# Constant products in TensorE's planned waits, a norm's sums on TensorE, and inverse square roots as powers on GpSimd

## The chip, the cores and the metric

The kernel runs on one NeuronCore of a Trainium2 chip. The core has five engines that run their own instruction queues in order and wait for one another by semaphores: TensorE (PE in the profile, with its weight loads listed as PEld), VectorE (DVE), ScalarE (ACT), GpSimd (POOL) and SyncE (SP), which here only issues DMAs. The metric is the device time of one execution in microseconds; the kernel before took 3143.68 us, the median of 3 runs from 3141.57 to 3146.34.

## What is computed

Two transformer blocks run one after the other on 512 tokens of 1024 features (the second block puts 16 learned tokens in front, so 528). All is float32. The first block has depth 2, each layer made of a gated feed-forward (FFN), a mixer of sliding-window attention and retention, and another FFN, every one followed by a layer norm. The second block has depth 1: FFN, a mixer of differential attention and of attention over tokens picked by an index score, and an FFN, with RMS norms ahead of each. Cut to what the change touches:

```
x = layer_norm(ALPHA * x + 0.5 * swiglu_ffn(x, ...), ln3_g, ln3_b)        # last of block 1
h = concatenate([meta_tokens, x]);  h = h + 0.5 * swiglu(rmsnorm(h, ffn1_norm), ...)   # first of block 2
layer_norm: (x - mean) * rsqrt(var + 1e-5) * g + b
rmsnorm:     x * rsqrt(mean(x * x) + 1e-6) * g
multiscale_retention:  o = (o - mu) * rsqrt(var + 1e-6)          # per head, 64 wide
mixer 2: qa, ka = rmsnorm per 64;  c, q_lat = rmsnorm per 256;  o_a = rmsnorm per 128
```

## The kernel before

**Layout.** Activations lie as 128 partitions (features) by tokens, `Z[128, 8, 528]`: 8 feature blocks, and the token axis is worked in two halves. Every float32 product with a weight is made of three products in the faster fp32r format (`mm3`): the weight and the activation are each split into a high and a low part, high*high, high*low and low*high add up in PSUM. The weights come by DMA one 128x1024 tile at a time (`wraw`), ScalarE writes the high part (`wsplit`), VectorE or GpSimd subtracts to get the low one. In the FFNs some products use a scheme with 7 products instead of 8 of half-size blocks, whose operands are sums of blocks (`turned`, `sums`).

**Who sets the order.** The Python program that writes the instructions keeps a plan: a clock for every engine (`plan.t["P"]` is TensorE's), a cost for every instruction (`Plan.COST`, and in `Engine` 0.1085 us or 0.000422 us per column for an fp32r product) and the end of every access to every tile. Work that hangs on other engines is written as jobs, Python generators that yield whenever their next step has to wait. The main program issues products; after each it calls `tick()`, which issues the weight preparation and every job step whose time has come on TensorE's planned clock (`run_due`). Where the main program can't go on (no free PSUM bank in `have`, or a condition in `until`), nothing is due, and the planned clock of TensorE is set forward to the next due time: the plan foresees a wait there. Since every engine runs its queue in order, the plan fixes the order of all instructions for good; on the chip an instruction starts when its semaphores allow.

**PSUM.** There are 8 banks in three rooms: `acc` (4), `s` (2) and `m` (2).

**The norms.** `Norm` gathers the sums of a norm while the products that make `Z` are still running. For each feature block and half, `_acc` squares `Z` on ScalarE and adds to the partial sums in SBUF. The kind "ln" keeps two sums (x and x*x), "rms" one. The kind "both" stands between the two blocks: a layer norm followed at once by an RMS norm, whose sum of squares is worked out from five sums (x, x*g*g, x*g*b, x*x, x*x*g*g) so that the tokens need only one pass; `wts` holds g*g and g*b. `stats` adds up over partitions with products with `ones` in TensorE, gets the inverse square roots, `bcast` spreads them over partitions with products with the unit matrix (`m<-identf,st`), and `apply` scales the 8 feature blocks (two VectorE products with PSUM, ScalarE for g and b, a further VectorE product with the RMS gain, and the split into high and low parts `x`).

**The inverse square root.** `rsqrt` is an integer guess of the bit pattern and two polynomial steps, 7 small VectorE instructions in a row, each on the one before; the constant KAPPA folds a scale into what it is given. It is used in the norms' `stats` (tile `st`, 2 or 3 columns), in retention's `group_norm` (8 columns), and in the second mixer for `qa` and `ka` (8 columns), the compressed keys (1), the latent queries (2) and the attention's output (4).

**Stages by time of the profile.** FFN 0 to 345 us, mixer 345 to 600, the first norm's hand-over to the next FFN 600 to 660, FFN to 945, FFN to 1300, mixer to 1595, hand-over to 1660, FFN to 1940, the "both" norm and the hand-over to block 2 from 1940 to 2090, FFN to 2345, second mixer 2425 to 2700, its output and norm to 2810, last FFN to the end.

Of the kernel before, what the change touches and what calls it, by code (L numbers as in the profile page):

```python
# [19 lines left out]
KAPPA = 13.375  # L20
R1, R2 = (-0.9039771828045722, 1.7085235438039765), (-4.244243335422951, 5.270893790588845)
# [4 lines left out]
MORE, TAIL = 1, 3  # L26
# [253 lines left out]
class Plan:  # L280
# [11 lines left out]
    def cost(self, e, name, n, reads, writes, kw, scalars):  # L292
        a, b = self.COST[e]
        if e == "S":
# [162 lines left out]
def build(ctx, tc, t, out, stop=None, dbg=None):  # L457
# [74 lines left out]
    V.memset(mean128, 1.0 / 128)  # L532
    ones = const.tile([128, 2], F32, name="ones")
# [83 lines left out]

    def until(done):
        while not done():
            W.advance()  # L620
            W.pump()
            if not run_due() and not done():
                plan.t["P"] = max(plan.t["P"], min(due(j) for j in eligible()))
# [32 lines left out]
    class Norm:  # L656
# [5 lines left out]
        def __init__(self, kind, halves, g=None, b=None, rms=None, xo=0):  # L662
# [3 lines left out]
            self.more = []  # L666
# [15 lines left out]
        def _acc(self, m, h):  # L682
# [30 lines left out]
            if self.kind == "both":  # L713
                add(self.more[2], q, 0)
# [14 lines left out]
        def z(self, m, *halves):  # L729

            if self.s2 is None:
                if self.kind == "both":
                    lt = main.tile([128, 4, 512], F32, name="lt", tag="V")
                    self.s1, self.s2 = lt[:, 0], lt[:, 1]
                    self.more = [lt[:, 2], lt[:, 3], have(tmps, (128, 512))]
# [20 lines left out]
        def stats(self, half):  # L756
# [6 lines left out]
            p = yield from want(ms, (128, 5, 3, 32))  # L763
            sums = [(j, u) for j, u in enumerate([self.s1, self.s2, *self.more]) if u is not None]
            for i, (c, w) in enumerate(tk):
                for j, u in sums:
                    PE.matmul(p[:w, j, i, 0:2], u[:, c:c + w], ones, start=True, stop=True)
            S1, S2, S1g, S1b, S2g = (p[:, j, 0:nt, 0] for j in range(5))
            if self.kind == "rms":
                if short < 128:  # L770
                    V.memset(v, 1.0)
                V.tensor_scalar(v[:, :full], S2[:, :full], KAPPA / 1024, KAPPA * 1e-6, op0=OP.mult, op1=OP.add)
                if full < nt:
                    V.tensor_scalar(v[:short, full:], S2[:short, full:], KAPPA / 1024, KAPPA * 1e-6, op0=OP.mult, op1=OP.add)
# [1740 lines left out]
```

## Time and profile before

| what | value |
| --- | --- |
| median of 3 runs | 3143.68 us |
| the profiled execution | 3140.53 us, span of its instructions 3138.8 us, so 1.7 us lie around the span |
| mean granted TensorE clock | 0.974 of full |
| TensorE busy | 3017.5 us, 96%, 20218 products |
| TensorE idle | 3138.8 - 3017.5 = 121.3 us |
| VectorE busy | 2240.9 us, 71% |
| ScalarE busy | 1368.0 us, 44% |
| GpSimd busy | 534.6 us, 17%, 360 instructions |
| share of the chain that ended last | PE 43%, DVE 8%, issue 3%, ACT 1% |

The granted clock has two levels, 1.2 and 2.4 GHz, shown as 0.5 and 1.0; a mean in between tells how much of a stretch was spent at each. A wait is shown at the end of a row as the idle time of the engine before the instruction and who ended it. An instruction of the program that multiplies float32 as it is (not fp32r) shows as two products in the trace: the program has 56 of `m<-ones,lt`, the trace 112.

### The profile page before, as it was taken

Reading aid. Unit: us, or ns where it says so; the run is one execution under the profiler, and the core shown is the slowest. Engines: PE = TensorE matmul, PEld = TensorE weight load, DVE = VectorE, ACT = ScalarE, POOL = GpSimd, SP = SyncE. Lnnn points to the kernel's source line nnn. Section 1 sums busy time; section 2 is a strip of 40 time slices with the busy share of each in tenths; the row PEclk is TensorE's granted clock in tenths of the full one; section 3 lists DMA queues with packets and bytes.
Section 4 is the critical chain, followed back from the end, with each engine's and each line's share of the span. In section 5 each row is a group of like instructions: output and inputs, shape, how many; then the busy total and the mean of one; then the engine's idle time right before and its main releaser. Section 6 shows DMA issues by size and latency. Waiting matters only on the chain.

```text
span 3138.8 us, 51092 instructions
## 1 busy us (share of the span) xinstructions
PE 3017.5 (96%) x20218; PEld 2739.3 (87%) x20218; DVE 2240.9 (71%) x4654; ACT 1368.0 (44%) x2517; POOL 534.6 (17%) x360
## 2 busy tenths in 40 slices
PE   8999999999999999999989999789999998999999
PEld 8999877789999999987779999789999677789997
DVE  6767655687677766775678668877675898577774
ACT  4444464354345433456344334243344345543342
POOL 1121222112212122022221221111102000212110
PEclk9999999999999999999999999899999997899999
DMA  4333221212323233311212323023332110122332
GB/s 145 108 101 103 87 89 61 74 61 95 102 101 102 95 101 102 127 61 61 68 48 84 105 101 128 22 72 99 101 108 89 56 58 21 34 78 97 101 101 88
DMA packets 75551, 269.71 MB, mean 86 GB/s; under 512 B 8445, under 2 KB 10533, under 8 KB 75184
## 3 DMA queue, kind: packets, MB, share of 16 engines
q1 hardware_dynamic: 73712, 261.65, 25.3%
q0 software_dynamic: 1024, 3.75, 0.4%
q8 instruction: 159, 2.61, 0.4%
q10 hardware_dynamic: 576, 1.05, 0.1%
q14 instruction: 80, 0.66, 0.1%
HBM read 264.30 MB, written 3.68 MB: 85 GB/s over the span
## 4 chain that ended last, share of the span: by engine, by line
PE 43%; DVE 8%; issue 3%; ACT 1%; POOL 0%; DMA 0%; DVEq 0%; ACTq 0%; POOLq 0%
PE acc L429 38%; PE m L429 2%; PE s L429 2%; DVE tmp L429 2%; DVE wsplit L429 1%; DVE Z L429 1%; DVE rsq L429 1%; DVE small L429 1%; DVE lt L429 1%; DVE sel L429 1%; ACT wsplit L429 0%; ACT tmp L429 0%; DVE turned L429 0%; DVE st L429 0%; POOL wsplit L429 0%
## 5 line engine op out<-in xcount | busy, mean ns | idle before, releaser
L429 PE MATMUL acc<-x,wsplit 128*128 128x256 f32 (+3 forms) x4248 | 607.7, 295 | 40.4 <-ACT x L429 17.8
L429 PEld LDWEIGHTS acc<-x,wsplit 128*128 128x128 f32 x4248 | 562.0, 194 | 60.1 <-ACT x L429 19.4
L429 ACT ACTIVATE wsplit<-wraw 128x1024 fp32r<-128x1024 f32 (+1 forms) x455 | 423.8, 947 | 384.0 <-PE acc L429 335.1
L429 PE MATMUL acc<-turned,wsplit 128*128 128x256 f32 (+1 forms) x4320 | 565.3, 283 | 8.6 <-DVE wsplit L429 6.3
L429 PEld LDWEIGHTS acc<-turned,wsplit 128*128 128x128 f32 x4320 | 541.0, 189 | 16.8 <-DVE wsplit L429 8.7
L429 DVE TENSOR_TENSOR wsplit<-wraw,wsplit 128x1024 fp32r<-128x1024 f32 (+1 forms) x376 | 402.3, 1074 | 132.1 <-ACT wsplit L429 130.1
L429 PE MATMUL acc<-H,wsplit 128*128 128x512 f32 (+2 forms) x2490 | 463.7, 339 | 5.0 <-DVE H L429 2.7
L429 PEld LDWEIGHTS acc<-H,wsplit 128*128 128x128 f32 x2490 | 380.3, 189 | 56.0 <-DVE H L429 4.8
L429 POOL TENSOR_TENSOR wsplit<-wraw,wsplit 128x1024 fp32r<-128x1024 f32 x79 | 193.5, 2449 | 1138.2 <-ACT wsplit L429 1030.2
L429 DVE TENSOR_TENSOR Z<-Z,acc 128x512 f32<-128x512 f32 (+2 forms) x295 | 165.7, 563 | 272.8 <-PE acc L429 272.0
L429 PE MATMUL acc<-wsplit,x 128*128 128x512 f32 (+3 forms) x1536 | 354.1, 381 | 0.0
L429 DVE TENSOR_TENSOR tmp<-tmp,acc 128x256 f32<-128x256 f32 (+1 forms) x570 | 238.7, 419 | 141.2 <-PE acc L429 133.8
L429 PEld LDWEIGHTS acc<-wsplit,x 128*128 128x128 f32 (+1 forms) x1536 | 261.4, 187 | 58.3 <-issue 1.2
L429 ACT ACTIVATE tmp<-acc 128x256 f32<-128x256 f32 (+4 forms) x282 | 110.0, 392 | 326.7 <-PE acc L429 313.0
L429 PE MATMUL acc<-H,turned 128*128 128x256 f32 (+2 forms) x1416 | 244.1, 327 | 0.0
L429 PEld LDWEIGHTS acc<-H,turned 128*128 128x128 f32 x1416 | 208.3, 191 | 20.6
L429 POOL TENSOR_TENSOR lent<-wraw,lent 128x1024 fp32r<-128x1024 f32 x45 | 110.9, 2464 | 595.3 <-ACT lent L429 572.7
L429 ACT ACTIVATE wsplit<-sums 128x1024 fp32r<-128x1024 f32 x90 | 95.3, 1059 | 236.7 <-DVE sums L429 236.3
L429 PE MATMUL acc<-x,lent 128*128 128x256 f32 (+1 forms) x1032 | 136.9, 281 | 0.0
L429 PEld LDWEIGHTS acc<-x,lent 128*128 128x128 f32 x1032 | 130.8, 188 | 2.4
L429 DVE TENSOR_TENSOR wsplit<-sums,wsplit 128x1024 fp32r<-128x1024 f32 x88 | 107.5, 1221 | 19.6 <-ACT wsplit L429 19.5
L429 DVE TENSOR_TENSOR sums<-wraw 128x512 f32<-128x512 f32 x173 | 119.4, 690 | 1.3
(327 smaller groups left out, 4133.3 us busy)
## 6 DMA issues: line engine op xcount, KB each, us to landing
wraw<-in_w_dram SPq DMA_DIRECT2D x489, 512.0 KB, 3.3
decay<-in_decay_dram SPq DMA_DIRECT2D x4, 512.0 KB, 4.9
vr<-vr POOLq DMA_DIRECT2D x1, 1536.0 KB, 8.1
Z<-in_x_dram SPq DMA_DIRECT2D x4, 256.0 KB, 6.2
Z<-in_x_dram SPq DMA_DIRECT2D x2, 512.0 KB, 12.5
tb<-vr POOLq DMA_DIRECT2D x2, 512.0 KB, 4.3
out_dram<-Z SPq DMA_DIRECT2D x4, 256.0 KB, 2.0
out_dram<-Z ACTq DMA_DIRECT2D x4, 256.0 KB, 2.0
```

Of the source, the lines that this page charges most:

```text
L429: r = f(*args, **kw)
```

## The change

Four things change.

- **Filled waits.** Where `have` or `until` set TensorE's planned clock forward, they now call `idle(upto)`. It takes a free PSUM bank and issues `n = wait * 0.8 / 0.118` products of the constant tile `minus` (128 rows by 256 columns, fp32r), whose result nobody reads, if n is at least 2. In all 491 of them in 40 places.
- **The "both" norm's sums.** `_acc` no longer adds five sums in SBUF. For every feature block, half and 128 tokens it makes two float32 products with `Z` and with its square as the stationary operand and four and two columns of `wts` as the moving one, adding up over the 8 feature blocks in one PSUM bank (`s`). `stats` reads the sums there, and the products with `ones` go for this norm.
- **rsqrt.** One GpSimd instruction, a power with exponent -0.5, in place of the 7 VectorE ones. KAPPA goes. In the plan it costs 0.4 + 0.156 us per column.
- **A yield behind rsqrt.** The jobs now give up their turn behind it, so that VectorE's next step of the job is issued when the plan says that the power is done.

```diff
-MORE, TAIL = 1, 3
+MORE, TAIL, WARM = 1, 3, 0.8
...
     def cost(self, e, name, n, reads, writes, kw, scalars):
         a, b = self.COST[e]
+        if kw.get("op") == OP.pow:
+            return 0.4 + 0.156 * n
...
             if not run_due():
-                plan.t["P"] = min([at] + [due(j) for j in eligible() if due(j) > now])
+                idle(min([at] + [due(j) for j in eligible() if due(j) > now]))
...
+    def idle(upto):
+
+        n = int((upto - plan.t["P"]) * WARM / 0.118)
+        rooms = [r for r in (ms, ss, accs) if r.open and r._at(r.open[0]) <= plan.t["P"]]
+        if n > 1 and rooms:
+            p = rooms[0].take((128, 512), F32)
+            for _ in range(n):
+                PE.matmul(p[:, :256], minus[:, 0:1].to_broadcast([128, 128]), minus[:, 0:1].to_broadcast([128, 256]),
+                          start=True, stop=True)
+            drop(p)
+        plan.t["P"] = max(plan.t["P"], upto)
...
     def rsqrt(v, n, rows=128, out=None):
 
-        y, q, a = (main.tile([128, n], F32, name="rsq", tag="rsq" + u, bufs=2)[:rows] for u in "yqa")
-        y = y if out is None else out
-        V.tensor_scalar(y.bitcast(I32), v.bitcast(I32), -0.5, float(0x5F3759DF), op0=OP.mult, op1=OP.add)
-        V.tensor_mul(q, y, y)
-        V.tensor_mul(q, q, v)
-        V.scalar_tensor_tensor(a, q, R1[0], q, op0=OP.add, op1=OP.mult)
-        V.scalar_tensor_tensor(q, q, R2[0], q, op0=OP.add, op1=OP.mult)
-        V.scalar_tensor_tensor(y, a, R1[1], y, op0=OP.add, op1=OP.mult)
-        V.scalar_tensor_tensor(y, q, R2[1], y, op0=OP.add, op1=OP.mult)
+        y = main.tile([128, n], F32, name="rsq", tag="rsq", bufs=6)[:rows] if out is None else out
+        G.tensor_tensor(y, v, power[:rows].to_broadcast([rows, n]), op=OP.pow)
         return y
...
+            if self.kind == "both":
+                q = yield from want(tmps, (128, n))
+                S.activation(q, z, AF.Square)
+                yield
+                for i, (t0, w) in enumerate(self.toks(h)):
+                    p = self.s2[:w, 2 * h + i]
+                    t0 -= c0
+                    PE.matmul(p[:, 0:4], z[:, t0:t0 + w], wts[:, m, 0:4], start=not self.begun, stop=m == 7,
+                              skip_group_check=True)
+                    self.begun.add(h)
+                    PE.matmul(p[:, 4:6], q[:, t0:t0 + w], wts[:, m, 0:2], start=False, stop=m == 7,
+                              skip_group_check=True)
+                drop(q)
+                self.taken[h] += 1
+                return
...
-            def add(d, a, col):
-                w = wts[:, m, col:col + 1]
-                if first:
-                    V.tensor_scalar(d[:, c0:c1], a, w, None, op0=OP.mult)
-                else:
-                    V.scalar_tensor_tensor(d[:, c0:c1], a, w, d[:, c0:c1], op0=OP.mult, op1=OP.add)
-
-            if self.kind == "both":
-                add(self.more[0], z, 0)
-                add(self.more[1], z, 1)
-            yield
-            if self.kind == "both":
-                add(self.more[2], q, 0)
+            yield
...
             rsqrt(v, nt, out=r)
             if self.kind != "rms":
+                yield
                 V.tensor_mul(mr, r, mu)
```

TensorE's queue at the end of the FFN ahead of block 2, the difference between the two programs; `m<-minus` are the constant products, `m<-Z,mean` is the mean of the first feature block, which the norm subtracts. The same two pieces stand at the end of the two FFNs before it.

```order
 L429 MATMUL acc<-x,wsplit 128x256 x12
 L429 MATMUL acc<-H,turned 128x512 x12
+L429 MATMUL m<-minus 128x256 x14
 L429 MATMUL acc<-H,wsplit 128x512 x24
+L429 MATMUL m<-minus 128x256 x7
 L429 MATMUL m<-Z,mean_94 128x512
```

Fourteen constant products now stand between the last down product of one chunk and the 24 products that need the last gated tile `H`, and seven ahead of the mean.

TensorE's queue at the "both" norm, before: the products that make the second half of `Z` stand on either side of the five sums' products with `ones` (4 on `lt` and 1 on `tmp` for each 128 tokens).

```order
L429 MATMUL acc<-H,wsplit 128x256 x24
L429 MATMUL acc<-tmp,minus 128x256
L429 MATMUL acc<-H,turned 128x256 x6
L429 MATMUL m<-ones,lt 128x2 x4
L429 MATMUL m<-ones,tmp 128x2
...
L429 MATMUL acc<-H,turned 128x256 x18
```

The same place now: the first of the 64 products with `wts` are put in between the products that make `Z`, as soon as the plan has a feature block ready.

```order
L429 MATMUL m<-Z,mean_94 128x512
L429 MATMUL acc<-H,wsplit 128x256 x21
L429 MATMUL s<-wts,Z 128x4
L429 MATMUL s<-wts,tmp 128x2
...
L429 MATMUL acc<-H,wsplit 128x256 x3
L429 MATMUL acc<-tmp,minus 128x256
```

They moved from one place behind each half into pairs strewn along the products of both halves, and there are 64 where 20 were.

VectorE's queue in the second mixer, before: the norm of a 128-token piece of `ka`, from the sum over squares (`TENSOR_REDUCE`) to the product with the result; `sel` are the index scores.

```order
L429 TENSOR_REDUCE small<-tmp 128x8
L429 TENSOR_SCALAR small<-small 128x8
L429 TENSOR_SCALAR rsq<-small 128x8
L429 TENSOR_TENSOR rsq<-rsq 128x8
L429 TENSOR_TENSOR rsq<-rsq,small 128x8
L429 SCALAR_TENSOR_TENSOR rsq<-rsq 128x8 x4
L429 TENSOR_TENSOR tmp<-acc,rsq 128x512
```

The first two such pieces now, on the same engine:

```order
L429 TENSOR_REDUCE small<-tmp 128x8
L429 TENSOR_SCALAR small<-small 128x8
L429 SCALAR_TENSOR_TENSOR sel_24648<-tmp,iw,sel_24648 128x528 x2
...
L429 TENSOR_TENSOR tmp<-acc,rsq 128x512
L429 MAX small<-sel_24646 128x8
L429 MATCH_REPLACE sel_24646<-small,sel_24646 128x272
```

Seven instructions are gone from between, and other work of VectorE stands there while GpSimd takes the power; two such pieces now run one in the other, and the bank `acc` is held until `tmp<-acc,rsq`. In this mixer TensorE's queue has 153 constant products, the largest groups 51 and 25, both among the `ka` and `va` products.

## Rows read from the trace of the kernel before

**Rows 1.** The page: busy time by engine, and the granted clock in 40 slices.
```profile
PE 3017.5 (96%) x20218; PEld 2739.3 (87%) x20218; DVE 2240.9 (71%) x4654; ACT 1368.0 (44%) x2517; POOL 534.6 (17%) x360
...
PEclk9999999999999999999999999899999997899999
```
**Rows 2.** Busy time by stretch: length, then PE, PEld, DVE, ACT, POOL, clock, DMA.
```profile
600.00:660.00 60.00, 51.24 (x336) 47.03 (x335) 49.34 (x132) 26.45 (x54) 11.32 (x8) 0.90 0.18 62
...
1660.00:1940.00 280.00, 279.19 (x1982) 261.75 (x1981) 201.73 (x315) 114.62 (x170) 53.01 (x28) 1.00 0.31 103
1940.00:2090.00 150.00, 120.66 (x837) 116.26 (x836) 122.74 (x310) 57.42 (x107) 20.70 (x16) 0.85 0.16 54
2425.00:2560.00 135.00, 125.23 (x638) 97.28 (x638) 116.75 (x319) 56.22 (x118) 6.39 (x3) 0.97 0.20 67
2560.00:2700.00 140.00, 124.21 (x668) 102.67 (x669) 112.52 (x411) 73.62 (x219) 15.43 (x15) 0.80 0.11 35
...
1595.00:1660.00 65.00, 56.10 (x413) 53.58 (x412) 57.82 (x166) 35.67 (x81) 13.84 (x12) 0.92 0.21 66
```
**Rows 3.** TensorE's waits from 1940 to 2090 us: total, times, longest.
```profile
PE s L429 <- ACT x L429: 8.4, 1, 8.4
PE acc L429 <- ACT tmp L429: 7.3, 2, 4.6
PE m L429 <- DVE lt L429: 6.3, 2, 4.6
PE acc L429 <- ACT x L429: 5.2, 1, 5.2
```
**Rows 4.** VectorE's groups by shape, 1955 to 2035 us: count, total, mean ns.
```profile
L429 DVE SCALAR_TENSOR_TENSOR lt<-Z,wts,lt 128x256 f32<-128x256 f32 x28 | 14.2, 547 | 0.0
...
L429 DVE SCALAR_TENSOR_TENSOR tmp<-tmp,wts 128x256 f32<-128x256 f32 x14 | 8.7, 624 | 0.0
...
L429 DVE TENSOR_TENSOR lt<-lt,Z 128x256 f32<-128x256 f32 x14 | 5.8, 412 | 0.0
L429 DVE TENSOR_TENSOR lt<-lt,tmp 128x256 f32<-128x256 f32 x14 | 5.8, 411 | 0.0
```
**Rows 5.** Timeline, the norm between the blocks: start, duration, what, count.
```profile
1970.09 2.99 PE L429 MATMUL acc<-H,wsplit 128*128 128x256 f32 x24
...
1971.36 2.81 POOL L429 TENSOR_TENSOR wsplit<-wraw,wsplit 128x1024 fp32r<-128x1024 f32 x1 [16.52 <-ACT wsplit L429]
...
1971.83 2.61 DVE L429 SCALAR_TENSOR_TENSOR tmp<-tmp,wts 128x256 f32<-128x256 f32 x1
...
1982.30 1.85 PE L429 MATMUL m<-ones,lt 128*128 128x2 f32 x8
...
2015.72 0.95 PE L429 MATMUL m<-ones,lt 128*128 128x2 f32 x8
```
**Rows 6.** Timeline of TensorE, the end of the first FFN.
```profile
326.68 5.07 PE L429 MATMUL acc<-H,wsplit 128*128 128x512 f32 x14 [1.37 <-DVE H L429]
```
**Rows 7.** The same at the end of the FFN ahead of block 2.
```profile
1945.33 3.51 PE L429 MATMUL acc<-H,wsplit 128*128 128x512 f32 x14 [0.18 <-DVE H L429]
1948.68 1.02 PE L429 MATMUL m<-Z,mean 128*128 128x512 f32 x2
```
**Rows 8.** The same at the start, and in the last FFN.
```profile
7.11 2.71 PE L429 MATMUL acc<-x,wsplit 128*128 128x256 f32 x11 [0.71 <-DVE x L429]
...
22.96 14.21 PE L429 MATMUL acc<-x,wsplit 128*128 128x256 f32 x118 [0.98 <-DVE wsplit L429]
...
3097.01 0.49 PE L429 MATMUL acc<-H,wsplit 128*128 128x512 f32 x1 [0.54 <-ACT H L429]
```
**Rows 9.** TensorE's waits from 2300 to 2425 us, the end of the fifth FFN.
```profile
PE acc L429 <- ACT H L429: 1.5, 1, 1.5
```
**Rows 10.** Timeline of VectorE, one inverse square root in the second mixer.
```profile
2462.77 0.17 DVE L429 TENSOR_SCALAR rsq<-small 128x8 int32<-128x8 int32 x1
...
2464.12 0.69 DVE L429 TENSOR_TENSOR tmp<-acc,rsq 128x512 f32<-128x512 f32 x1
```
**Rows 11.** TensorE's waits from 2425 to 2560 us, the first half of the second mixer.
```profile
PE m L429 <- DVE tmp L429: 8.4, 7, 3.3
```
**Rows 12.** TensorE's waits from 2560 to 2700 us, its second half.
```profile
PE m L429 <- ACT tmp L429: 4.8, 3, 2.6
PE acc L429 <- ACT tmp L429: 4.1, 2, 2.5
```
**Rows 13.** GpSimd's groups by shape: count, total, mean ns.
```profile
L429 POOL TENSOR_TENSOR wsplit<-wraw,wsplit 128x1024 fp32r<-128x1024 f32 x79 | 193.5, 2449 | 1138.2 <-ACT wsplit L429 1030.2 <-PE m L429 35.8 <-DVE small L429 32.9
...
L429 POOL TENSOR_TENSOR tmp<-tmp 128x128 f32<-128x128 f32 x8 | 3.7, 456 | 18.6 <-DVE tmp L429 14.8 <-issue 3.7
...
L429 POOL TENSOR_TENSOR tmp<-tmp 128x256 f32<-128x256 f32 x2 | 1.5, 732 | 11.1 <-ACT tmp L429 11.1
```

More of the change, by code (lines that the diff above doesn't have):

```diff
@@ L19 @@
 NPT = 6
-KAPPA = 13.375
-R1, R2 = (-0.9039771828045722, 1.7085235438039765), (-4.244243335422951, 5.270893790588845)
 SIDE = 2
@@ L532, in build @@
     V.memset(mean128, 1.0 / 128)
+    power = const.tile([128, 1], F32, name="power")
+    V.memset(power, -0.5)
     ones = const.tile([128, 2], F32, name="ones")
@@ L622, in until @@
             if not run_due() and not done():
-                plan.t["P"] = max(plan.t["P"], min(due(j) for j in eligible()))
+                idle(min(due(j) for j in eligible()))
     def drain():
@@ L665, in __init__ @@
             self.s1 = self.s2 = self.c = None
-            self.more = []
             self.wait, self.full, self.begun, self.first = [], set(), set(), set()
@@ L732, in z @@
                 if self.kind == "both":
-                    lt = main.tile([128, 4, 512], F32, name="lt", tag="V")
-                    self.s1, self.s2 = lt[:, 0], lt[:, 1]
-                    self.more = [lt[:, 2], lt[:, 3], have(tmps, (128, 512))]
+                    self.s2 = have(ss, (128, 4, 8))
                 elif self.kind == "ln":
@@ L762, in stats @@
             a, v, r, mr, R = (st[:, i] for i in range(5))
[L763 to L768, printed above, removed]
+            if self.kind == "both":
+                S1, S1g, S1b, S2, S2g = (self.s2[:, 2 * half:2 * half + 2, j] for j in (0, 1, 2, 4, 5))
+            else:
+                p = yield from want(ms, (128, 2, 3, 32))
+                sums = [(j, u) for j, u in enumerate([self.s1, self.s2]) if u is not None]
+                for i, (c, w) in enumerate(tk):
+                    for j, u in sums:
+                        PE.matmul(p[:w, j, i, 0:2], u[:, c:c + w], ones, start=True, stop=True)
+                S1, S2 = (p[:, j, 0:nt, 0] for j in range(2))
             if self.kind == "rms":
@@ L771, in stats @@
                     V.memset(v, 1.0)
-                V.tensor_scalar(v[:, :full], S2[:, :full], KAPPA / 1024, KAPPA * 1e-6, op0=OP.mult, op1=OP.add)
+                V.tensor_scalar(v[:, :full], S2[:, :full], 1.0 / 1024, 1e-6, op0=OP.mult, op1=OP.add)
                 if full < nt:
-                    V.tensor_scalar(v[:short, full:], S2[:short, full:], KAPPA / 1024, KAPPA * 1e-6, op0=OP.mult, op1=OP.add)
+                    V.tensor_scalar(v[:short, full:], S2[:short, full:], 1.0 / 1024, 1e-6, op0=OP.mult, op1=OP.add)
             else:
@@ L777, in stats @@
                 V.tensor_scalar(mu, S1, 1.0 / 1024, None, op0=OP.mult)
-                V.scalar_tensor_tensor(a, mu, KAPPA, mu, op0=OP.mult, op1=OP.mult)
-                V.scalar_tensor_tensor(v, S2, KAPPA / 1024, a, op0=OP.mult, op1=OP.subtract)
-                V.tensor_scalar(v, v, KAPPA * 1e-5, None, op0=OP.add)
+                V.tensor_mul(a, mu, mu)
+                V.scalar_tensor_tensor(v, S2, 1.0 / 1024, a, op0=OP.mult, op1=OP.subtract)
+                V.tensor_scalar(v, v, 1e-5, None, op0=OP.add)
             rsqrt(v, nt, out=r)
             if self.kind != "rms":
+                yield
                 V.tensor_mul(mr, r, mu)
@@ L792, in stats @@
                 V.tensor_mul(u, u, r)
-                V.tensor_scalar(u, u, KAPPA / 1024, tot[:, 2:3], op0=OP.mult, op1=OP.add)
+                V.tensor_scalar(u, u, 1.0 / 1024, tot[:, 2:3], op0=OP.mult, op1=OP.add)
                 rsqrt(u, nt, out=R)
-            drop(p)
+            if self.kind != "both":
+                drop(p)
             self.st = r, mr, R
@@ L846, in run @@
             if half == 1 and self.kind != "ln":
-                drop(self.s2 if self.kind == "rms" else self.more[2])
+                drop(self.s2)
             yield
@@ L1667, in both_prep @@
         V.memset(u, 0.0)
-        V.tensor_mul(wts[:, :, 0], g, g)
-        V.tensor_mul(wts[:, :, 1], g, b)
-        V.tensor_copy(u[:, :, 0:2], wts)
+        V.memset(wts[:, :, 0:4:3], 1.0)
+        V.tensor_mul(wts[:, :, 1], g, g)
+        V.tensor_mul(wts[:, :, 2], g, b)
+        V.tensor_copy(u[:, :, 0:2], wts[:, :, 1:3])
         V.tensor_mul(u[:, :, 2], b, b)
@@ L1704, in meta_apply @@
         drop(y)
-    wts = main.tile([128, 8, 2], F32, name="wts")
+    wts = main.tile([128, 8, 4], F32, name="wts")
     tot = main.tile([128, 3], F32, name="tot")
@@ L1953, in steps @@
                 V.tensor_reduce(v, a, axis=mybir.AxisListType.X, op=OP.add)
-                V.tensor_scalar(v, v, KAPPA / 64, KAPPA * 1e-6, op0=OP.mult, op1=OP.add)
+                V.tensor_scalar(v, v, 1.0 / 64, 1e-6, op0=OP.mult, op1=OP.add)
                 r = rsqrt(v, 8, n)
+                yield
                 V.tensor_mul(a, pv, r[:, :, None].to_broadcast([n, 8, 64]))
@@ L2061, in sub_norm @@
             V.tensor_reduce(v, q, axis=mybir.AxisListType.X, op=OP.add)
-            V.tensor_scalar(v, v, KAPPA / 128, KAPPA * 1e-6, op0=OP.mult, op1=OP.add)
+            V.tensor_scalar(v, v, 1.0 / 128, 1e-6, op0=OP.mult, op1=OP.add)
             r = rsqrt(v, 4)
+            yield
             V.tensor_mul(o, o, r[:, :, None].to_broadcast([128, 4, 128]))
@@ L2103, in latent_key @@
             yield
-            V.tensor_scalar(v, v, KAPPA / 256, KAPPA * 1e-6, op0=OP.mult, op1=OP.add)
+            V.tensor_scalar(v, v, 1.0 / 256, 1e-6, op0=OP.mult, op1=OP.add)
             r = rsqrt(v, 1, n)
+            yield
             S.activation(a, p[:n, :256], AF.Copy, scale=r)
@@ L2165, in latent @@
             yield
-            V.tensor_scalar(v, v, KAPPA / 256, KAPPA * 1e-6, op0=OP.mult, op1=OP.add)
+            V.tensor_scalar(v, v, 1.0 / 256, 1e-6, op0=OP.mult, op1=OP.add)
             r = rsqrt(v, 2)
+            yield
             for j in range(2):
```

8 lines of the change are left out of this document (4 added, 4 removed).

## The prediction

> **What bounds the kernel now.** I read the page first. TensorE is busy for 3017.5 us of the span [rows 1], so the whole game is the 121.3 us in which it is idle and the time that it works at the lower of its two clock levels. The clock line of the page shows that the low level is not spread evenly: it dips at the hand-overs and most in one slice past the middle of block 2 [rows 1]. The table by stretch then says where: inside an FFN TensorE is busy for 279.19 of 280 us at 1.00, so nothing but fewer products helps there. The "both" norm is at 120.66 of 150 us and 0.85, the second mixer at 125.23 of 135 (0.97) and 124.21 of 140 (0.80), the hand-overs after the two first mixers at 51.24 of 60 (0.90) and 56.10 of 65 (0.92) [rows 2]. A mean clock c means that 2(1-c) of the stretch was at half speed, and a product that runs then takes twice its time, so the excess is at most half of that, times the busy share: 45 us x 0.80 / 2 = 18 for the norm, 56 x 0.89 / 2 = 25 and 8 x 0.93 / 2 = 4 for the two halves of the mixer, 12 x 0.85 / 2 = 5 and 10 x 0.86 / 2 = 4 for the hand-overs. Last I read the waits of these stretches, which say who is late.
>
> **Prices.** At full clock 24 products of 128x256 take 2.99 us, 0.12 us each [rows 5]; a constant product has this shape. At the low clock 11 of the same took 2.71 us, 0.25 each [rows 8]. A small float32 product counts as two: eight of `m<-ones,lt` took 0.95 us at full and 1.85 us at low clock [rows 5], so one of the program costs 0.24 or 0.46 us.
>
> **The "both" norm.** Gone from VectorE are four groups, 14.2 + 8.7 + 5.8 + 5.8 = 34.5 us of its 80 [rows 4], of which it was busy for 122.74 in the 150 [rows 2]. What TensorE waited for there: 6.3 us for `lt`, 5.2 and 8.4 for `x`, 7.3 for the `tmp` that turns operands for the next FFN [rows 3]. The first goes with `lt`. The `x` waits are VectorE's and ScalarE's apply, which stood behind the sums; I let 5.2 and 5.4 of the 8.4 go. The 7.3 stay: apply and turning are unchanged work and are late next. That is -16.9 us. Of the 18 us of excess I give back 10, since a long wait stays. Added are 64 products of the program for 20: 64 x 0.24 = 15.4 less 20 x 0.24 = 4.8, so +10.6 us of TensorE, nearly all of it between products that make `Z`, where nothing hides it. Of the 60 constant products ahead of the next FFN, 7.2 us, I count half as standing beyond the wait that they fill: +3.6. Sum: -16.9 - 10 + 10.6 + 3.6 = -12.7 us.
>
> One VectorE row there, a 128x256 product of 2.61 us, stands against a mean of 0.62 for its kind [rows 4, 5], and GpSimd's 2.81 us `wsplit` runs beside it [rows 5]. The Trainium skill says the same in "GPSIMD Engine Reference", section "8. Key points": the two engines share an interface to SBUF. Were every GpSimd power to hold VectorE up for its own length, the relief in the mixer (below) would shrink from 35 us to about 35 - 26 x 0.73 = 16, which is why I give the rival that lives on that relief less than it would have otherwise.
>
> **Constant products at the ends of the FFNs.** There are 136, in 12 places: 136 x 0.12 = 16.3 us. The waits that they stand for were 1.37 us [rows 6], 0.18 [rows 7] and two more of that size, 1.5 [rows 9], 0.54 [rows 8], and none ahead of the mean, whose row has no wait at all [rows 7]: about 3.9 us together. TensorE's queue is in order, so what the wait doesn't cover is paid: +12.4. The clock that they can save is little, as an FFN's end mostly is at full clock [rows 2]: -1.7. Sum +10.7 us.
>
> **Start.** 66 constant products run ahead of the first real ones. The products from 7.11 us run at the low clock, yet what ends this stretch is the 0.98 us wait for VectorE's `wsplit` at 22.96 [rows 8]; faster products would only wait longer. I take 0.
>
> **Hand-overs after the two first mixers.** 76 constant products, 9.1 us, against 8.8 + 8.9 us of idle [rows 2]. Two thirds of them inside it cost 0, one third +3; of the 9 us of excess 6 come back. -3 us.
>
> **Second mixer.** The 153 constant products are 153 x 0.12 = 18.4 us against 9.8 + 15.8 = 25.6 us of idle and 25 + 4 = 29 us of excess [rows 2]. The inverse square roots here are 26 of the program's 53; one is 2464.12 - 2462.77 = 1.35 us of VectorE [rows 10], so VectorE loses 35 us of 229 [rows 2]. The trace of before has no power on GpSimd. Bounds by GpSimd's nearest rows: 0.456 us for 128x128 and 2.449 for 128x1024, both far wider than the 128x8 here [rows 13]; I take 0.73, the row of 128x256, since a power is more than a subtraction but the tile is small, and two hand-overs between engines on top. So a root is about as long as before (from 0.9 us shorter to 1.1 longer in the chain), and with 26 on a chain of waits the ends are -23 and +29; what is surely gained is VectorE's time. It has company: TensorE waited for `tmp` from VectorE for 8.4 us in seven pieces [rows 11]. With planned waits on such a scale and a plan that only guesses their place, I let half of the idle time be filled or fall (-13), a third of the excess go (-9) and charge the 18.4: -3.6 us.
>
> A power queued behind a GpSimd `wsplit` would wait for up to 2.449 us, but GpSimd is busy for 6.39 + 15.43 of 275 us here [rows 2], so one in twelve. The roots of the norms elsewhere, and retention's, lie beside products that run on; 0.
>
> **Sum.** -12.7 + 10.7 + 0 - 3 - 3.6 = -8.6 us. The profiled execution took 3140.5 us (span and 1.7 around it), 3.2 below the median of the runs; it would become 3131.9, and a median of 3135.
>
> **The rivals.**
> - *The relief carries the mixer.* VectorE, busy for 229 of 275 us, is what the mixer really hangs on; 35 us less lets `tmp` come in time, the constant products hold the clock, and idle and excess both fall to a quarter: -19 -22 + 18.4 = -23 in place of -3.6, so -28 in all; I round for what then waits on ScalarE (4.8 + 4.1 us there now, [rows 12]) to -25, 3118 us. For it: the 8.4 us [rows 11]. Against: a third of the idle time there is ScalarE's.
> - *The constant products stand ahead of work that is ready.* Slower. On TensorE they go first and can't be recalled; the plan's waits are not the chip's, as the FFN ends show, where 14 products stand for 0.18 us [rows 7]. If only a fifth of the 153 falls into idle time and the clock doesn't come back, the mixer is at +12; with +11 from the ends and -8 from the norm that is +15, 3158 us. It decides from the point where under a third of the 153 lie in idle time.
> - *The power is dear.* If GpSimd takes 3 us for 128x8, longer than its longest row, each of the 26 roots comes 1.7 us late, half of them on the path: +22, and 3166 us. The point is 1.35 us of VectorE plus what a hand-over takes back, some 1.5 us. Against: seven instructions of 1.35 / 7 = 0.19 us become one, and none of GpSimd's rows is near 3 us [rows 13]. The Trainium skill speaks for it: "GPSIMD Engine Reference", section "4.1 Engine selection", would keep elementwise work on VectorE, with GpSimd about twice as slow for two operands. By that one instruction of VectorE's kind would be some 0.4 us here, an estimate by that page.
> - *It doesn't do what it says.* Products of a broadcast constant neither raise nor hold the clock: only their 491 x 0.12 = 59 us remain, of which idle time takes some 40, and the norm's -16.9 + 10.6: about +13, 3157 us.
>
> **How the numbers follow.** Chances: forecast 0.40, its own range 3122 to 3147 (the mixer's idle share filled by a quarter or by three quarters, the norm's 60 products inside or outside the wait); relief 0.22; products in the way 0.22; dear power 0.10; no effect on the clock 0.06. A measurement of this kernel can tell 0.2%, 6.3 us, from no change. "Faster" is three fifths of the forecast (its middle is 8.6 below) and all of the relief: 0.46. "Same" is most of the rest of the forecast and a little of the second and last rivals: 0.23. "Slower" is 0.31. For 8 in 10 the range goes from 3112 (relief, with half as much again in the other hand-overs) to 3160 (products in the way); outside lie the dear power and the far end of the relief.
>
> **What the profile after would show.** Right: no wait on `lt` and a wait for `x` under 4 us between 1940 and 2090; that stretch some 13 us shorter, its clock above 0.90; each FFN end about 2 us longer, with the constant products followed by no wait; GpSimd rows of a power near 0.73 us; the second mixer about level, at clock above 0.90. Wrong: a root from sum to product of over 2.5 us; a mixer where constant products are followed by further waits as long as before; a clock that still falls in spite of them; or a norm between the blocks whose `x` is as late as before, which would mean that ScalarE, not VectorE, had held it.

## The result, and the profile after

The changed kernel takes 3107.16 us, the median of 4 runs from 3105.4 to 3108.15; before took 3142.62 (4 runs, 3137.3 to 3146.34). The ratio is 0.989, with an interval from 0.9877 to 0.9903: 35 us less, outside the range of 3112 to 3160 and four times the 8.6 us that were forecast. The page of the changed kernel, to be read against [rows 1]:

```profile
PE 3043.5 (98%) x20797; PEld 2770.7 (89%) x20797; DVE 2149.0 (69%) x4209; ACT 1366.7 (44%) x2517; POOL 585.6 (19%) x411
...
PEclk9999999999999999999999999999999999999999
```

TensorE is busy for 26.0 us more and the span is 3103.5 us, 35.3 less, so its idle time fell from 121.3 to 60.0 us. The clock line has no dip left. Adding up the stretches of 1 us, where a mean clock c stands for 2(1-c) at the low level, the time that products lost there falls from 66.0 to 25.1 us. Together 102 us were freed and 35 gained, so 67 were spent. By their prices the 491 constant products at 0.12 (59 us) and the norm's 64 products (14.3, less the 4.8 of the 20 that went) come to 68.

To say where, I cut both traces at the same products: the mean ahead of each norm, the first `acc<-H,lent` of the FFN behind the norm between the blocks, the first `s<-ikT,iqT` of the second mixer and the first `acc<-yA,wsplit` behind its last `s<-yB,lent`. Lengths in us, for the profiled execution of each kernel (the experiments are told below):

| kernel | span | "both" norm | second mixer | 2nd of the first mixers | all else |
| --- | --- | --- | --- | --- | --- |
| before | 3138.8 | 147.0 | 313.8 | 280.1 | 2397.9 |
| after | 3103.5 | 124.9 | 294.7 | 285.7 | 2398.2 |
| e1 no constant products | 3111.5 | 127.2 | 297.7 | 284.0 | 2402.6 |
| e2 constant products alone | 3133.8 | 138.9 | 312.3 | 280.8 | 2401.8 |
| e3 sums alone | 3120.2 | 130.8 | 313.0 | 279.0 | 2397.4 |
| e4 powers alone | 3113.8 | 136.3 | 295.1 | 284.0 | 2398.4 |
| e5 powers, VectorE's load kept | 3147.1 | 135.2 | 338.0 | 277.4 | 2396.5 |
| e6 yields alone | 3131.1 | 138.8 | 322.1 | 275.8 | 2394.4 |
| e7 powers in mixer 2 alone | 3115.6 | 144.9 | 294.9 | 282.4 | 2393.4 |
| e8, e11 better kernel | 3097.4, 3092.9 | 125.2, 125.3 | 294.7, 294.7 | 281.1, 278.3 | 2396.4, 2394.6 |

Of the 35 us, 22.1 lie in the norm between the blocks and 19.1 in the second mixer; the second of the first mixers got 5.6 longer. The busy times of the two stretches (length, then PE, PEld, DVE, ACT, POOL, clock, DMA), before:

```profile
1948.68:2095.71 147.03, 117.87 (x847) 115.39 (x846) 119.52 (x307) 54.31 (x105) 21.42 (x17) 0.85 0.17 54
2440.53:2754.33 313.80, 287.64 (x1531) 232.55 (x1530) 242.15 (x789) 147.35 (x382) 28.76 (x28) 0.90 0.12 39
```

and after:

```profile
1952.49:2077.38 124.89, 122.58 (x997) 120.94 (x996) 81.03 (x201) 52.67 (x104) 17.48 (x20) 0.97 0.19 61
2420.96:2715.70 294.74, 286.89 (x1684) 236.11 (x1682) 213.52 (x609) 147.55 (x382) 52.56 (x52) 0.98 0.13 42
```

The third busy time is VectorE's: 38.5 us less in the norm, 28.6 less in the mixer. TensorE's idle time is 2.3 us where it was 29.2, and 7.9 where it was 26.2; the clock went from 0.85 to 0.97 and from 0.90 to 0.98. All that TensorE still waited for between the blocks, in answer to [rows 3]:

```profile
PE acc L429 <- ACT x L429: 1.4, 1, 1.4
PE acc L429 <- POOL x L429: 0.4, 1, 0.4
PE acc L429 <- DVE tmp L429: 0.4, 1, 0.4
```

The 7.3 us for `tmp`, which I had left in place, are gone too. 60 constant products of 7.17 us stand in this stretch now, but they are not what took that wait away: in e1, which has none, TensorE waits there for `tmp` for 0.6 us. The end of the FFN ahead of the norm, TensorE's timeline (start, duration), in answer to [rows 7], and the first of the new sums:

```profile
1944.55 1.73 PE L429 MATMUL m<-minus 128*128 128x256 f32 x14
1946.12 5.76 PE L429 MATMUL acc<-H,wsplit 128*128 128x512 f32 x24
...
1951.71 0.94 PE L429 MATMUL m<-minus 128*128 128x256 f32 x7
1952.49 1.02 PE L429 MATMUL m<-Z,mean 128*128 128x512 f32 x2
...
1955.83 0.28 PE L429 MATMUL s<-wts,Z 128*128 128x4 f32 x2
1955.96 0.36 PE L429 MATMUL s<-wts,tmp 128*128 128x2 f32 x2
...
1957.97 0.36 PE L429 MATMUL s<-wts,Z 128*128 128x4 f32 x2
```

The 21 constant products hold the queue for (1946.12 - 1944.55) + (1952.49 - 1951.71) = 2.35 us for a wait of 0.18, near the forecast. What a power costs on GpSimd (count, total, mean ns):

```profile
L429 POOL TENSOR_TENSOR rsq<-small,power 128x8 f32<-128x8 f32 x16 | 31.2, 1954 | 134.0 <-DVE small L429 133.9
L429 POOL TENSOR_TENSOR st<-st,power 128x2 f32<-128x2 f32 x16 | 11.5, 721 | 145.1 <-DVE st L429 145.1
...
L429 POOL TENSOR_TENSOR rsq<-small,power 128x4 f32<-128x4 f32 x4 | 4.1, 1019 | 22.0 <-DVE small L429 21.9
```

That of 128x8 takes 1.95 us on average, not 0.73, and is longer than VectorE's 1.35 [rows 10]. The mean mixes two kinds. Six begin with no VectorE `TENSOR_TENSOR` or `SCALAR_TENSOR_TENSOR` under way and take 1.64 to 1.71 us, like the first here; ten begin while one with two inputs runs and take 1.88 to 2.71, like the second, which begins inside an instruction of 0.76 us:

```profile
599.53 1.64 POOL L429 TENSOR_TENSOR rsq<-small,power 128x8 f32<-128x8 f32 x1 [6.44 <-DVE small L429]
...
2443.27 2.08 POOL L429 TENSOR_TENSOR rsq<-small,power 128x8 f32<-128x8 f32 x1 [36.09 <-DVE small L429]
```

Of the 26 roots of the second mixer nine have 8 columns; the other 17 take 0.53 to 1.04 us as powers and some 1.2 on VectorE, and all 26 together 30.0 us in place of 33.9. So the 8-column roots got longer, the others shorter, and the mixer became 19 us shorter. Whether that came from the roots' own length, from VectorE's lighter queue or from the constant products was the question for the runs.

### The profile page after: what moved, and what is told of

Same layout as the page of the kernel before. It is cut to its first block, busy times and chain, and to the rows that moved or that the text cites. A ratio compares the mean times of both kernels' runs of the same rounds, so it can differ in the third digit from the quotient of the medians.

```text
span 3103.5 us, 51892 instructions
## 1 busy us (share of the span) xinstructions
PE 3043.5 (98%) x20797; PEld 2770.7 (89%) x20797; DVE 2149.0 (69%) x4209; ACT 1366.7 (44%) x2517; POOL 585.6 (19%) x411
## 4 chain that ended last, share of the span: by engine, by line
PE 73%; DVE 3%; issue 2%; ACT 2%; POOL 1%; DMA 0%; ACTq 0%; POOLq 0%; DVEq 0%
PE acc L429 65%; PE m L429 4%; PE s L429 4%; DVE wsplit L429 1%; DVE tmp L429 1%; DVE Z L429 1%; ACT wsplit L429 0%; POOL wsplit L429 0%; ACT tmp L429 0%; DVE x L429 0%; ACT Z L429 0%; POOL rsq L429 0%; DMA tb<-vr 0%; ACT x L429 0%; DVE y L429 0%
## 5 line engine op out<-in xcount | busy, mean ns | idle before, releaser
L429 PE MATMUL acc<-x,wsplit 128*128 128x256 f32 (+3 forms) x4248 | 598.0, 291 | 15.2 <-POOL x L429 5.3
L429 PEld LDWEIGHTS acc<-x,wsplit 128*128 128x128 f32 x4248 | 551.8, 190 | 35.1 <-POOL x L429 7.0
L429 PEld LDWEIGHTS acc<-turned,wsplit 128*128 128x128 f32 x4320 | 538.5, 189 | 16.2 <-DVE wsplit L429 9.5
L429 POOL TENSOR_TENSOR wsplit<-wraw,wsplit 128x1024 fp32r<-128x1024 f32 x74 | 180.5, 2439 | 912.8 <-ACT wsplit L429 847.4
L429 ACT ACTIVATE tmp<-acc 128x256 f32<-128x256 f32 (+2 forms) x278 | 108.6, 393 | 311.6 <-PE acc L429 301.4
```

The lines of the kernel that those rows point to most:

```text
L429: r = f(*args, **kw)
```

## The experiments

Theory 1 was that the constant products hold the clock in waits that are there anyway; theory 2 that a shorter VectorE queue takes the waits away. Each run's time is the median of its timed runs, and its ratio is to runs of before on the same chip; that chip is another one for e5 to e8 (before takes 3139.27 us there, 3142.65 beside e1 to e4 and 3138.07 beside e9 to e12), so runs are compared by their ratios.

**e1: no constant products.** `-MORE, TAIL, WARM = 1, 3, 0.8` / `+MORE, TAIL, WARM = 1, 3, 0.0`

> The changed kernel without any constant product (the norm's sums on TensorE and the powers stay; the plan sets the clock forward over the same waits). Theory 1, the constant products hold TensorE's clock and stand almost wholly in waits that are there anyway: taking them away makes it slower, by the clock's excess that comes back in the second mixer and at the hand-overs, some 15 to 25 us, so 3122 to 3132 us, with the mixer's mean clock back near 0.90. Theory 2, the shorter VectorE queue (sums gone, roots gone) took the waits away: then the constant products were 58 us of TensorE for nothing, and without them it stays at 3107 or falls to 3095.

3111.58 us, ratio 0.9902 (0.989 to 0.9915): 4.4 us slower than with them, with intervals that overlap. Neither theory had that. The second mixer:

```profile
2423.38:2721.12 297.74, 281.86 (x1531) 229.47 (x1530) 213.69 (x609) 147.93 (x382) 52.51 (x52) 0.93 0.12 41
```

The clock does come back down to 0.93, so the constant products hold it as theory 1 says; but the 22 us of idle time and low clock that they save there cost 18.4 us of TensorE, and 3 us remain. Even these are not sure: e9 and e10 below keep the 153 constant products of this mixer, and it takes 297.5 and 297.6 us there.

**e2: constant products alone,** `idle()` and its two calls added to the kernel before.

> The kernel before with the constant products alone (its sums and roots as they were). Theory 1: the excess at the low clock falls by half or more in the second mixer and the hand-overs, 20 us, and the idle time that it fills costs nothing: 3122 to 3130 us. Theory 2: the waits stay, the constant products that miss them cost: 3143 to 3155 us.

3135.54 us, ratio 0.9983 (0.9974 to 0.9992): -7 us, between the two ranges. In the profiled execution, 5.0 us shorter, the norm between the blocks is 8.1 shorter, the second mixer 1.5, and the rest 4.6 longer. The second mixer:

```profile
2436.44:2748.73 312.29, 290.33 (x1640) 237.08 (x1639) 242.00 (x789) 146.95 (x382) 28.79 (x28) 0.95 0.12 40
```

The idle time is 4.2 us less than before and the clock is up from 0.90 to 0.95, yet 109 constant products (13 us at 0.12) take most of that back. Without the powers the constant products do little here.

**e3: the sums alone,** the changed kernel with WARM at 0 and VectorE's seven instructions for every root.

> The norm's sums on TensorE alone, no powers and no constant products. Both theories: the wait for lt and most of the waits for x go between the blocks, -12 to -24 us, so 3119 to 3131 us, and everything behind the norm is shifted with its own length as before. If the norm's gain needed the constant products or the powers, it is under 8 us: above 3135.

3124.32 us, ratio 0.9944 (0.9932 to 0.9955), as expected. The norm's stretch is 130.8 us, 16.2 less; the second mixer is as before. The norm's stretch:

```profile
1946.56:2077.33 130.77, 119.75 (x935) 117.28 (x934) 90.37 (x229) 53.18 (x105) 17.13 (x17) 0.95 0.19 61
```

**e4: the powers alone,** on the kernel before:

```diff
-KAPPA = 13.375
+KAPPA = 1.0
...
+        G.tensor_tensor(y, v, power[:rows].to_broadcast([rows, n]), op=OP.pow)   # for the seven of VectorE
...
             r = rsqrt(v, 8)
+            yield
```

> The powers on GpSimd alone (and the yields behind them). Theory 1: a 128x8 power takes 1.95 us on GpSimd in the changed kernel's trace against 1.35 for the seven VectorE instructions, so a chain gets longer while VectorE gets freer: 3138 to 3150 us, second mixer no shorter than before by more than 4 us. Theory 2: the second mixer gets 15 to 20 us shorter, 3122 to 3128 us.

3116.86 us, ratio 0.9923 (0.9911 to 0.9935): -26 us, the largest of the three parts. The mixer's gain is theory 2's number, the total lies below its range. The norm's stretch and the second mixer:

```profile
1949.34:2085.66 136.32, 113.88 (x847) 112.08 (x846) 115.73 (x280) 52.84 (x105) 21.40 (x20) 0.89 0.17 58
2432.66:2727.78 295.12, 277.57 (x1530) 225.84 (x1529) 213.78 (x609) 147.52 (x382) 51.81 (x52) 0.94 0.13 42
```

The mixer loses 18.7 us with no constant product in it: 8.6 of idle time, and 10.1 of TensorE's busy time, which is the same 1530 products at a clock of 0.94 for 0.90. The waits of TensorE that fell are those that ScalarE ended, from 10.5 to 0.5 us, while those that VectorE ended stay (14.9 and 16.1). Most of ScalarE's had themselves stood behind a root on VectorE, as here before:

```profile
2640.66 0.84 ACT L429 ACTIVATE tmp<-acc,rsq 128x256 f32<-128x256 f32 x2 [3.48 <-DVE rsq L429]
2641.19 1.11 PE L429 MATMUL acc<-identf,tmp 128*128 128x128 f32 x4 [1.57 <-ACT tmp L429]
```

That left open whether VectorE's queue is shorter or only better ordered.

**e5: powers, with VectorE's load kept.** Ahead of the power in e4, the same seven instructions into a scratch tile `t`:

```diff
+        V.tensor_scalar(t.bitcast(I32), v.bitcast(I32), -0.5, float(0x5F3759DF), op0=OP.mult, op1=OP.add)
+        V.tensor_mul(q, t, t)
...
+        V.scalar_tensor_tensor(t, q, R2[1], t, op0=OP.add, op1=OP.mult)
         G.tensor_tensor(y, v, power[:rows].to_broadcast([rows, n]), op=OP.pow)
```

> The powers on GpSimd as in the run before (3117 us), but VectorE still issues the seven instructions of each root, into a scratch tile that nobody reads, ahead of the power. Theory 2a, the gain is VectorE's 1.35 us per root that others in its queue no longer stand behind: it goes back to 3138 to 3146 us, the second mixer to 310 to 316 us (295 with powers alone, 314 before). Theory 2b, the gain is that the root leaves the queue's order (its result is fetched later, other work goes between): it stays at 3117 to 3124 us, the mixer at 295 to 300.

3151.06 us, ratio 1.0038 (1.0024 to 1.0053): 36 us slower than e4 by the ratios, and slower than before. That is 2a's direction, but the time and the mixer's length lie above its ranges. The mixer and its two longest waits:

```profile
2421.16:2759.13 337.97, 295.91 (x1531) 242.96 (x1530) 247.66 (x789) 148.34 (x382) 51.64 (x54) 0.86 0.11 37
```
```profile
PE m L431 <- DVE tmp L431: 15.2, 2, 9.7
PE s L431 <- ACT tmp L431: 8.8, 3, 8.3
```

With 33.9 us more of VectorE the mixer is 42.9 us longer than in e4, the clock's share included: the powers' gain is gone when VectorE keeps its load. It isn't the length of a root that costs, as the first one shows (`load` are the scratch tiles):

```profile
2443.18 0.17 DVE L431 TENSOR_SCALAR small<-small 128x8 f32<-128x8 f32 x1
2443.39 0.17 DVE L431 TENSOR_SCALAR load<-small 128x8 int32<-128x8 int32 x1
2443.43 1.64 POOL L431 TENSOR_TENSOR rsq<-small,power 128x8 f32<-128x8 f32 x1 [36.08 <-DVE small L431]
...
2449.78 0.68 DVE L431 TENSOR_TENSOR tmp<-acc,rsq 128x512 f32<-128x512 f32 x1
```

The power begins 0.08 us behind its input, as in e4, and is done at 2445.07, but the product that needs it begins at 2449.78: VectorE does other work first. From the begin of an 8-column root to its product it is 4.2 to 9.8 us here and 2.0 to 4.4 in e4. Nor are the 42.9 us the price of the load alone, since the plan made another order: of VectorE's 606 instructions here besides the scratch ones, 431 stand in the order of e4. e4's order with the load kept was not run, so how much is load and how much order stays open.

**e6: yields alone,** the kernel before with the yields behind VectorE's roots.

> The kernel before with only the yields behind the roots: same instructions on every engine, VectorE's seven per root included, but the plan may put other VectorE work between a root and its use. Theory 2a: no gain, 3139 to 3146 us. Theory 2b: most of the 26 us, 3117 to 3127 us.

3135.06 us, ratio 0.9988 (0.9979 to 0.9998), between the two ranges. The second mixer is 8.3 us longer than before, so this order gives nothing there. The norm between the blocks, though, is 8.2 us shorter. Both stretches:

```profile
1940.95:2079.78 138.83, 114.01 (x847) 111.85 (x846) 120.23 (x307) 53.03 (x105) 19.83 (x17) 0.89 0.18 57
2424.86:2747.00 322.14, 292.34 (x1531) 236.53 (x1529) 240.05 (x789) 147.65 (x382) 26.63 (x28) 0.89 0.12 38
```

**e7: powers for the 26 roots of the second mixer alone.**

> Powers only for the 26 roots of the second mixer; the norms and the first two mixers keep VectorE's roots. If the roots' gain sits where they are: the second mixer at 295 us (-19), the norm between the blocks back at 147 us, the second of the two first mixers back at 280 (-4 against all powers): 3120 to 3126 us. If the norm's 10.7 us came from a moved weight preparation that any change of the plan can bring, the norm's stretch can be anywhere from 136 to 147.

3116.1 us, ratio 0.9924 (0.9909 to 0.9939), below the range. The mixer is at 294.9 us, the whole gain; the norm's stretch at 144.9:

```profile
2436.00:2730.86 294.86, 277.57 (x1531) 226.03 (x1530) 213.85 (x609) 147.81 (x382) 52.53 (x52) 0.94 0.13 42
```

With e6 this says that most of the 10.7 us that e4 gained in the norm came with the yields there (8.2 in e6), not with the powers. The second of the first mixers is at 282.4, not 280, without any power in it: part of its length differs from program to program, and I claim only what e8 shows below.

**e8: a better kernel?** Two things undone:

```diff
-        if n > 1 and rooms:
+        if n > 1 and rooms and not any(a < plan.t["P"] < a + 15 for a in (295, 866, 1195, 1766, 2125, 2778)):
...
-            r = rsqrt(v, 8)
-            yield
+            r = rsqrt(v, 8, dve=True)       # group norm: the seven VectorE instructions
```

> The changed kernel with two things undone: no constant products at the ends of the six FFNs, and the roots of retention's group norm on VectorE again (the others stay powers). By the stretches of the runs so far: the two FFNs in the middle give back 1.9 each at most, the second of the first mixers 4: 3096 to 3103 us, against 3107. If the constant products at the FFN ends hold a clock that would fall, or the powers in the group norm cost nothing, 3106 to 3112.

3096.13 us, ratio 0.9866 (0.9846 to 0.9887), four times from 3090.3 to 3106.7: as expected, though e9 and e10 don't bear out the reasons.

**e9: only the first of the two. e10: only the second. e11: e8 again.**

> The changed kernel without the 123 constant products at the ends of the FFNs (368 stay); all roots are powers. If these are TensorE's own time and no more, 123 x 0.12 = 14.8 us less what waits they covered (3.9) and the clock (under 2): 3097 to 3102 us. If they hold the clock into the norms: 3105 to 3112.

> The changed kernel with retention's eight group-norm roots on VectorE again, all constant products as changed (475 by the plan's waits). The long power (1.95 us against 1.35) is late there: the second of the first mixers gives back 4 to 5 us: 3101 to 3104 us. If the plan's new order made those 5 us: 3106 to 3109.

> Both of these, as in the better kernel, a second time, since its four times lay 16 us apart: 3093 to 3099 us if its median was right, 3100 to 3104 if it had luck.

e9 3106.23 us, ratio 0.9893 (0.9878 to 0.9908), and e10 3106.97, 0.9897 (0.9882 to 0.9911): both are misses, no better than the changed kernel. e11: 3093.42, 0.9858 (0.984 to 0.9877). In e9 the third FFN does fall from 355.9 to 353.9 us and in e10 the second of the first mixers from 285.7 to 281.9; but both have a second mixer of some 297.5 us and a norm 2 us longer, with more lost to the low clock in all (37.8 and 32.4 us against 25.1). The second mixer there has the same instructions in the same order on VectorE, ScalarE and GpSimd as in the changed kernel. Why their clock fell in more places stays open. That falls also come and go with the same program is shown by e8 and e11, where the second of the first mixers took 281.1 and 278.3 us, with 4.7 and 0.0 us lost to the clock. Of the eight times of the better kernel six lie under 3100 us, and none of the changed kernel's; its gain over the changed kernel, 11 to 14 us by the medians and 8 to 10 by the ratios to before, is only known for the two edits together.

**e12: e8 without the 153 constant products of the second mixer.** `+ and not 2200 < plan.t["P"] < 2400`

> As the better kernel, without the 153 constant products of the second mixer. The clock's excess comes back there (19 us in the run without any, 5 with them) and so does the idle time (16 against 8), and 18 us of products go: the stretch 297 to 299 us against 295, 3098 to 3101 us in all. If the constant products are what the mixer's gain rests on, 3110 us or more; if they only cost, 3085.

3101.92 us, ratio 0.9885 (0.9866 to 0.9904); four times from 3096.7 to 3107.7. The mixer:

```profile
2411.32:2708.03 296.71, 279.41 (x1530) 227.19 (x1529) 213.50 (x609) 147.43 (x382) 52.48 (x52) 0.94 0.13 42
```

The stretch is 296.7 us, against 294.7 with them. The 2 us are less than what the mixer differs by with them (294.7 to 297.6), so in this mixer the constant products neither carry the gain nor cost anything that shows.

## Why the prediction was wrong

- **The second mixer: the step that failed.** "I let half of the idle time be filled or fall (-13), a third of the excess go (-9) and charge the 18.4: -3.6 us." Measured: idle time -18.3, excess -20.2, and the 18.4 as charged, so -19 to -20. The sum had no term for what VectorE's relief does to TensorE; the relief itself (35 us reckoned, 28.6 measured) was in the text. The runs show two steps. The powers, with the yields behind them, take away 8.6 us of idle time and 10.7 of excess at no price on TensorE, and the mixer is 18.7 us shorter (e4). The constant products then take away 8.0 and 14.3 (the changed kernel against e1) for their 18.4, so that little is left of them. The mechanism that I gave a chance of 0.22 is the one that runs: the mixer's gain comes with the powers (e4, e7), not with the constant products (e1, e2, e12) or with the yields alone (e6), and it is gone when VectorE keeps its load (e5). "A third of the idle time there is ScalarE's" did not speak against it, since ScalarE had waited for roots (e4).
- **Both sizes were needed to leave the range.** With the mixer's miss of 15.5 us alone the forecast of 3135 becomes 3119.5, inside it; with the norm's 9.4 as well it becomes 3110.
- **The caution that lowered that rival** did not hold. Of the 101 VectorE instructions that run beside a power in the changed kernel none is over 0.15 us longer than the median of its kind with GpSimd idle, as its timeline beside GpSimd's shows:

```profile
509.24 0.56 DVE L429 TENSOR_TENSOR pt<-tmp,pt 128x384 fp32r<-128x384 f32 x1
...
509.41 1.92 POOL L429 TENSOR_TENSOR rsq<-small,power 128x8 f32<-128x8 f32 x1 [2.93 <-DVE small L429]
509.71 0.42 DVE L429 TENSOR_TENSOR tmp<-s,decay 128x256 f32<-128x256 f32 x1
...
510.25 0.68 DVE L429 TENSOR_TENSOR pt<-tmp,pt 128x512 fp32r<-128x512 f32 x1
```

  The 128x512 instruction begins and ends inside the 1.92 us and takes 0.68. It is the power that is held up, 1.92 us for 1.64. The 2.61 us row of [rows 5] stood beside a 128x1024 subtraction, not beside a tile of 8 columns.
- **The norm between the blocks**, -12.7 forecast and -22.1 measured. The mechanism was right, and the sums alone bring -16.2 (e3). Mis-sized were the waits, -16.9 forecast and -26.9 measured, by what is late next: "The 7.3 stay". In e3 that wait is 0.6 us, with 3.1 for `turned` in its place; the rest of the 22 came from the constant products and the yields (e2 and e6 have 8 us of each, alone; they overlap, and the changed kernel without its constant products is 2.3 longer there, e1). A new product took (1957.97 - 1955.96) / 9 = 0.22 us, not 0.24.
- **The price of a power** was wrong by 1.2 us (1.95 for 0.73, inside the bounds of 0.456 and 2.449) and did not decide. It could have been read off: the plan's own price, 0.4 + 0.156 us per column, gives 1.65 for 8 columns, and 1.64 is what a power takes that nothing holds up. The rival "the power is dear" put its point at 1.5 us of latency for all 26 roots; nine are over it and 17 under, and the mixer is 19 us shorter. The sign against the forecast, "a root from sum to product of over 2.5 us", did come: the first power begins at 2443.27, its product at

```profile
2447.00 0.68 DVE L429 TENSOR_TENSOR tmp<-acc,rsq 128x512 f32<-128x512 f32 x1
```

  3.7 us later, and the loss that it was to announce did not. In the second of the first mixers something does come late, TensorE's wait growing from 3.36 us ahead of the product at 1516.53 before to the first row here; GpSimd's and VectorE's rows behind it say why:

```profile
1518.27 1.09 PE L429 MATMUL m<-identf,tmp 128*128 128x128 f32 x4 [5.50 <-DVE tmp L429]
...
1509.81 2.71 POOL L429 TENSOR_TENSOR rsq<-small,power 128x8 f32<-128x8 f32 x1 [2.48 <-DVE small L429]
1512.49 2.35 POOL L429 TENSOR_TENSOR lent<-wraw,lent 128x1024 fp32r<-128x1024 f32 x1
1514.79 2.79 POOL L429 TENSOR_TENSOR wsplit<-wraw,wsplit 128x1024 fp32r<-128x1024 f32 x1
...
1509.79 1.22 DVE L429 TENSOR_TENSOR wsplit<-wraw,wsplit 128x1024 fp32r<-128x1024 f32 x1
1512.56 2.83 DVE L429 TENSOR_TENSOR tmp<-tmp,rsq 128x512 f32<-128x512 f32 x1 [1.54 <-POOL rsq L429]
1515.42 2.71 DVE L429 TENSOR_TENSOR tmp<-tmp,sg 128x512 f32<-128x512 f32 x1
```

  The power takes 2.71 us beside VectorE's two-input `wsplit`, and the two products that wait for it (0.69 us each in the trace of before) then meet GpSimd's 128x1024 subtractions and take 2.83 and 2.71. The Trainium skill names this contention for VectorE instructions with two SBUF inputs ("GPSIMD Engine Reference", section "8. Key points"); these rows agree with it. Beside a power, though, the rows at 509 us show only the power held up.
- **The constant products at the FFN ends** were near in the one FFN where they can be read: in the third, which has the one pair of 14 and 7 and little else, +1.9 us measured against 2.5 - 0.2 = 2.3 by the sum. (The count of 136 had ten that stand ahead of the last FFN's hand-over and three more; e9 takes out 123, and as a whole is no faster for it.) Outside the norm and the second mixer the change costs 5.9 us; the sum had 10.7 - 3 = 7.7.
- **The rivals.** "The constant products stand ahead of ready work" is true in part. The first three rows here are of the changed kernel, the last two of e1 at the same place:

```profile
2444.00 5.88 PE L429 MATMUL m<-minus 128*128 128x256 f32 x51
2449.72 0.86 PE L429 MATMUL acc<-wsplit,x 128*128 128x512 f32 x3
2450.41 0.60 PE L429 MATMUL m<-identf,tmp 128*128 128x128 f32 x4
...
2446.43 0.86 PE L429 MATMUL acc<-wsplit,x 128*128 128x512 f32 x3
2450.16 0.66 PE L429 MATMUL m<-identf,tmp 128*128 128x128 f32 x4 [2.87 <-DVE tmp L429]
```

  Without the 51 constant products of 5.88 us the product behind them runs at once, and the wait for `tmp`, 2.87 us, comes one product later; so some 3 us of the 51 stand ahead of ready work. Over the mixer 8.0 of the 18.4 us fall into idle time (15.9 us in e1, 7.9 with them), over the third at which that rival was to decide, and the low clock gives back the rest. (Its +12 for the mixer would be 18.4 x 4/5 = 14.7 by its own condition.) "It doesn't do what it says" is wrong: the mixer's clock rose from 0.93 (e1) to 0.98. But that clock is bought with TensorE's own time, and the 2 to 3 us that are left (e12, e1) are no more than the mixer differs by between e9 and the changed kernel.

## What to carry to other kernels

Where one stretch shows idle time, a low clock and a feeding engine that is busy for three quarters of it or more, look for one cause: give the relief of the feeding engine a term of its own and let idle time and clock follow from it, before shading each by itself. Here 28.4 us less of VectorE brought 18.7 (e4), so about two thirds; the way back (e5) cost more than it took, in another order. An instruction that is slower on an idle engine can still win when it takes work from an engine that the stretch waits for; e5, which gave the load back and kept the rest, is the run that shows that the gain goes with it. Read who waited for the engine that ended a wait, too: most of ScalarE's here were waits for VectorE's roots. Filling waits with products buys back the clock at nearly the price of the products, so it pays only where the wait is real.

## What the runs showed of the hardware

- A GpSimd power with a broadcast exponent took 0.55, 0.70, 0.88, 1.01 and 1.64 us for 128 rows of 1, 2, 3, 4 and 8 columns where nothing held it up: about 0.16 us per column and 0.4 on top, where a product or sum of two 128x256 tiles takes 0.73 [rows 13].
- One of 8 columns that began while a two-input VectorE instruction of 0.56 to 0.76 us ran took 1.88 to 2.08 us, and 2.42 to 2.71 beside a VectorE `wsplit` of 1.22. The VectorE instructions beside powers kept their lengths.
- 153 constant products took the second mixer's mean clock from 0.93 to 0.98 (e1 and after); what they gained there beyond their own 18.4 us, 2 to 3 us, is not clear of the 3 us by which this mixer differs with them from program to program (e9, e10 and after).
